# Three early projections in place of six, split gates, and the late modulation's loads and the inversion's writes issued by ACT

## The chip, the cores and the metric

The kernel runs on one core of one Trainium2 chip. The metric is the time of one execution on the device, in microseconds (us). A core has five engines that work at once, each through its own instructions in order: PE (TensorE, matrix products), DVE (VectorE), ACT (ScalarE), POOL (GpSimd) and SP (SyncE). Transfers between device memory (DRAM) and on-chip memory run on 16 DMA engines. They are started by issue instructions, which stand in the order of the engine that issues them: here nearly all on SP.

## The reference, cut to what matters

Two layers over 256 context and 256 latent tokens (512 in all), 2048 channels. Layer 0 mixes with a bidirectional gated DeltaNet, layer 1 with differential attention. Before each layer the tokens are normalised and modulated, `h = rmsnorm(x) * (1 + sc) + sh`, and after it a residual is added with a gate `gt`. The vectors `sh`, `sc`, `gt` are thirds of `silu(c) @ ada_w + ada_b`, a 2048 by 6144 product for each layer and for each of two vectors, `c` and `c_ctx`.

```python
def project(h):
    qkv, z, ba = jnp.split(h @ w_in, [DN_CONV_CH, DN_CONV_CH + DN_VW], axis=-1)
    q, k, v = jnp.split(short_conv_silu(qkv, conv_w), [DN_QK, 2 * DN_QK], axis=-1)
    ...
    beta = jax.nn.sigmoid(ba[:, :, :, 0])
    g = -jnp.exp(a_log) * jax.nn.softplus(ba[:, :, :, 1] + dt_bias)
...
gc = jnp.cumsum(chunks(g), axis=-1)
decay = jnp.exp(gc[..., :, None] - gc[..., None, :])          # lower triangle
lower = strict(einsum(kb, kc) * decay)
tinv = triangular_solve(eye + lower, eye)
a_intra = einsum(qc, kc) * decay
# then a scan over the chunks: v_new = u - w S, o = q S + a_intra v_new, S = ...
```

## The kernel before, in words

**Tiling.** Layer 0 has 16 groups `g` of two value heads. A group needs six projections of the 512 tokens by 128 columns: `k`, `q`, `v0`, `v1`, `z0`, `z1`. Numbers are kept in two parts, a rounded `hi` and a rest `lo` (`split`, line 184: ACT casts the `hi` at line 185, POOL subtracts the `lo` at line 187), and each product is three matmuls. One projection is 16 tiles of the contracted channels times 3, so 48 matmuls of 128x512 on PE; the weights of group 0's `k` are called `g0k…`, and so on.

**Prologue (lines 259 to 325).** A first half of layer 0's modulation (`sh`, `sc`) comes from 64 loads `ar` of 512 KB and 256 groups of small matmuls (`ada_pair`, line 173). `make_h` (line 216) then writes the modulated tokens `hhi`, `hlo`, two tiles a step, POOL first, then ACT, then DVE; its factor `rrow` needs all 16 tiles `xt` of the input. In step with it run six early projections: `ba` (the input of the gates), `k0`, `q0`, `v00`, `v01` and group 1's `k1`. Their weights are loads `er` at line 308, cast and split like the others. The tile `rc` is `silu(c)`, written to DRAM as `sc_d` by an issue on ACT (line 324).

**Gates (line 375).** `gt_baT` takes over the projection `ba` (line 397), PE turns it, and a softplus of both halves at once (tiles 512 wide; reciprocal at line 420, a chain of seven steps at line 425) gives `g` (line 434) and `lnb`. `gc_d` takes the cumulated `g` to DRAM in four writes, and `gct` (line 440, finished at line 459) keeps it on chip. The small table `adt`, which the softplus needs at line 416, is loaded at line 371.

**The steady state.** `decay` (line 677) loads a piece of `gc_d` into the single buffer `grm` or `gra` (line 681), DVE subtracts (line 687), ACT takes the exponential (line 689), and `ma` or `at` (line 695) is a product with it. `block_inv` (line 698) inverts small triangles: it writes `m16` to `mb_d` (line 701), reads it back in another layout as `bk` (line 703), runs 15 steps `bP`, `bY` on DVE (lines 712, 714), casts `bT` on ACT (lines 717, 718) and writes it to `tu_d` (line 720). `stream_lev` (line 755) loads `T` and `U` from there (line 774) and doubles the inverse on PE, up to `uf` (line 790). With `uf`, `stream_b` runs the scan. `filler` (line 647) puts the remaining projections between these.

**Late modulation.** The rest of the modulation (`gt` of layer 0, all of layer 1) is cut into 1024 pieces. `ada_part` (line 133) loads `aw` (line 135, two buffers `ra`), POOL multiplies it by a copy `cr` of `silu(c)` (line 138, one buffer `rp`) and ACT sums the product (line 139). `cr` is loaded from `sc_d` at line 158.

**What sets the order.** Generators describe streams with priorities and model costs; a loop `Drive` (line 481 on) steps the one that is ready. `dr.set("tu", g, half, lat=32)` tells that loop that the inverse is there 32 us later. The framework then schedules the instructions of each engine by its own timeline and high-priority blocks. On the chip every engine keeps the order that came out.

```python
nc.sync.dma_start(r, d["adaw"][l, ct, :, q * NK:(q + 1) * NK])          # line 135
nc.gpsimd.tensor_tensor(pr, r, cr[:, s], ALU.mult)                       # line 138
nc.scalar.activation(pr, pr, AF.Copy, accum_out=acc[:, s, q:q + 1])      # line 139
```

Of the kernel before, what the change touches and what calls it, by code (L numbers as in the profile page):

```python
# [61 lines left out]
def body(ctx, tc, D, d, out):  # L62
# [208 lines left out]
    with tc.high_priority():  # L271
        ada_pair(0, 0, ada_load(0, 0, t0, "ar", 12), gq(), t0)
        xt = [hpool.tile([P, T], F32, tag="hlo", name=f"xt{kt}", bufs=KT) for kt in range(KT)]
        for kt in range(KT):
            nc.sync.dma_start(xt[kt], d["xT"][:, kt])
    with tc.high_priority():
        acc0 = t0.tile([P, T], F32, name="acc0")
        nc.scalar.activation(acc0, xt[0], AF.Square)
        for kt in range(1, KT):
            sq = t0.tile([P, T], F32, tag="mh", name=f"sq{kt}", bufs=2)  # L280
            nc.scalar.activation(sq, xt[kt], AF.Square)
            nc.vector.tensor_tensor(acc0, acc0, sq, ALU.add)
        rrow0 = t0.tile([P, T], F32, name="rrow0")
        nc.scalar.copy(rrow0, rstd_rows(acc0, T, lambda: so().rearrange("p a b i -> p (a b i)"),
                                         t0.tile([P, 4, P], F32, name="rr_dg0")))

    SK = 2
# [7 lines left out]
    np_ = 0  # L295
    for k0 in range(0, KT, SK):
        with tc.high_priority():
            for kind in range(2):
# [6 lines left out]
        for n, src, _ in EARLY:
            w = SK * P
            r = t0.tile([P, w], F32, tag="er", name=f"e{n}r{k0}", bufs=4)
            nc.sync.dma_start(r, src[:, k0 * P:k0 * P + w])
            hi = t0.tile([P, w], F32R, tag="eh", name=f"e{n}h{k0}", bufs=8)
            lo = t0.tile([P, w], F32R, tag="el", name=f"e{n}l{k0}", bufs=8)  # L310
            split(hi, lo, r)
            for k in range(SK):
                kt, ks = k0 + k, slice(k * P, (k + 1) * P)
                ps = early[n]
                mm(ps, hi[:, ks], hhi[:, kt, :], kt == 0, False)
                mm(ps, hi[:, ks], hl(kt), False, False)
                mm(ps, lo[:, ks], hhi[:, kt, :], False, kt == KT - 1)
    rc = t0.tile([2, D], F32, name="rc")
    nc.sync.dma_start(rc, d["crow"])
    rth = t0.tile([2, D], F32, name="rth")  # L320
    nc.scalar.activation(rth, rc, AF.Tanh, scale=0.5)
    nc.vector.scalar_tensor_tensor(rc, rth, 1.0, rc, ALU.add, ALU.mult)
    nc.vector.tensor_scalar(rc, rc, 0.5, None, ALU.mult)
    nc.scalar.dma_start(sc_d, rc)
# [31 lines left out]
    zt = dl.tile([P, 1024], F16, name="zt", tag="m16", bufs=4)  # L356
    nc.vector.memset(zt, 0.0)
    full = lambda a: a.rearrange("u (j i) -> j u i", i=P)[:P]
    diag = lambda a: bass.AP(tensor=a[:].tensor, offset=a[:].offset, ap=[[16 * P + 16, 64], [P, 16], [1, 16]])
    for i in range(2):  # L360
        for j in range(2):
            nc.sync.dma_start(full(tu_d[i][j]), zt.rearrange("p (u i) -> p u i", u=8))

    convw = load_small("convw", [P, 4 * KT, 5], d["convw"], dl)
    adt = load_small("adt", [P, 2, 2, HV], d["adt"].to_broadcast([P, NB]).rearrange("p (k d h) -> p k d h", k=2, d=2), dl)
    hh = lambda kt: hhi[:, kt, :]

    beta = dl.tile([P, NCH, 2, HV], F32, name="beta", tag="O", bufs=2)
    gct = dl.tile([P, NCH, 2, HV], F32, name="gct")
    eg = dl.tile([P, NCH, 2, HV], F32, name="eg")  # L370
    kd = dl.tile([P, NCH, 2, HV], F32, name="kd")
    egl = dl.tile([P, NCH, 2, HV], F32, name="egl")
# [922 lines left out]
```

## Time and profile before

| what | value |
|---|---|
| three runs, median (lowest to highest) | 3181.67 us (3176.39 to 3182.67) |
| the profiled execution, its own time | 3170.24 us |
| its span, first to last instruction | 3168.5 us |
| granted TensorE clock, mean over the span | 0.954 of full speed |
| PE, DVE, POOL, ACT busy | 89%, 62%, 64%, 59% of the span |
| first `uf` (end of the start-up) | 342.2 us |

The page and the answers of the trace are read in microseconds from the first instruction. "A <- B" after a wait names what ended it. A name ending in q (SPq, ACTq) is the engine's queue, where DMAs are issued; "busy" counts no issue time. Matmul records overlap by pipelining, so the distance between their starts tells the rate, and the record's own length does not.

### The profile page before, as it was taken

The page shows a single profiled execution, that of the slowest core. Times are in us where ns is not written, and L with a number is a line of the kernel's source. Part 1 is how long each engine was busy: PE and PEld are TensorE (multiplying, and loading weights), DVE is VectorE, ACT ScalarE, POOL GpSimd, SP SyncE. Part 2 cuts the span into 40 slices and gives each one's busy share as a digit, 9 for nine tenths or more (in the row PEclk, how much of TensorE's full clock was granted, in tenths as well). Part 3 has the DMA queues.
Part 4 walks back from the last instruction along what each step waited for, and adds up shares of the span by engine and source line. Part 5 has one row for each costly group of instructions (what it writes and reads, how often), then busy time and mean ns, then how long its engine had stood idle before and what let it go on. Part 6 is the DMA issues. An engine that isn't in the chain of part 4 may idle for free.

```text
span 3168.5 us, 52448 instructions
## 1 busy us (share of the span) xinstructions
PE 2833.0 (89%) x16178; PEld 2236.6 (71%) x16178; DVE 1980.1 (62%) x4274; ACT 1863.0 (59%) x5466; POOL 2026.2 (64%) x2370
## 2 busy tenths in 40 slices
PE   4977888888998988998988988899898999999998
PEld 1555666676776766776766766677686888888888
DVE  2148768778778688588688688632334664545454
ACT  3545666666766766766666666654455665434354
POOL 2567677777787777777777777566466677322234
PEclk6988999999999999999999999999999999999999
DMA  9645445455545555545455546656744454333345
GB/s 362 223 114 118 123 119 135 123 133 118 139 134 129 127 126 133 128 129 136 122 125 131 132 118 134 173 171 189 230 147 132 144 164 150 123 110 113 117 127 164
DMA packets 511795, 457.06 MB, mean 144 GB/s; under 512 B 241684, under 2 KB 383764, under 8 KB 511508
## 3 DMA queue, kind: packets, MB, share of 16 engines
q1 hardware_dynamic: 511508, 453.68, 51.8%
q8 instruction: 127, 2.08, 0.3%
q14 instruction: 156, 1.28, 0.1%
q10 hardware_dynamic: 4, 0.02, 0.0%
HBM read 427.18 MB, written 26.36 MB: 143 GB/s over the span
## 4 chain that ended last, share of the span: by engine, by line
PE 33%; DVE 26%; DMA 19%; ACT 7%; POOL 7%; issue 5%; SPq 2%; POOLq 0%; DVEq 0%; ACTq 0%
PE pj L83 28%; DMA gra<-gc_d 5%; POOL rp L138 4%; DMA grm<-gc_d 4%; DVE bP L712 4%; DVE grm L687 3%; DMA aw<-in_adaw_dram 3%; DVE gra L687 2%; DVE bY L714 2%; ACT rp L139 2%; DVE R L783 1%; PE sb L83 1%; DMA ar<-in_adaw_dram 1%; PE iv L83 1%; DVE ma L695 1%
## 5 line engine op out<-in xcount | busy, mean ns | idle before, releaser
L139 ACT ACTIVATE rp<-rp 128x256 f32<-128x256 f32 x1024 | 426.9, 417 | 378.6 <-POOL rp L138 375.5
L712 DVE TENSOR_TENSOR bP<-bX,bY 64x1 f32<-64x1 f32 (+14 forms) x480 | 228.8, 477 | 18.1 <-ACT bY L710 9.8
L139 ACT ACTIVATION_READ_ACCUMULATOR rp<-rp 128x1 f32 x1024 | 194.0, 189 | 0.0
L687 DVE TENSOR_SCALAR gra<-gra,gct,lnb 128x128 f32<-128x128 f32 x256 | 114.3, 488 | 97.9 <-DMA gra<-gc_d 97.2
L687 DVE TENSOR_SCALAR grm<-grm,gct,lnb 128x128 f32<-128x128 f32 x256 | 144.9, 610 | 47.9 <-DMA grm<-gc_d 47.3
L783 DVE TENSOR_TENSOR R<-iv,lv 128x512 f16<-128x512 f32 x192 | 126.1, 678 | 32.8 <-PE iv L83 32.6
L689 ACT ACTIVATE grm<-grm 128x512 f32<-128x512 f32 x64 | 40.4, 631 | 132.0 <-DVE grm L687 127.1
L83 PEld LDWEIGHTS <-m 128*128 128x128 f16 x1024 | 74.2, 100 | 62.0 <-issue 57.7
L714 DVE TENSOR_REDUCE bY<-bP 64x1 f32<-64x1 f32 (+14 forms) x480 | 108.8, 227 | 8.7
L83 PE MATMUL iv<-U,R 128*128 128x128 f16 x768 | 75.7, 223 | 34.4 <-DVE R L783 30.0
L83 PEld LDWEIGHTS <-R 128*128 128x128 f16 x768 | 47.6, 99 | 77.6 <-DVE R L783 44.6
L745 POOL TENSOR_TENSOR ma<-ma,cs 128x512 f32<-128x512 f32 x64 | 85.3, 1333 | 20.7 <-DVE ma L695 18.3
L83 PE MATMUL sb<-yb,uf 128*128 128x128 bf16 x512 | 54.2, 225 | 40.7 <-ACT yb L879 22.2
L689 ACT ACTIVATE gra<-gra 128x512 f32<-128x512 f32 x64 | 40.4, 631 | 84.1 <-DVE gra L687 84.1
L83 PE MATMUL iv<-T,m 128*128 128x128 f16 x768 | 71.4, 223 | 15.8 <-ACT T L800 7.2
L224 DVE TENSOR_TENSOR hlo<-mh,hhi 128x512 fp32r<-128x512 f32 x32 | 29.6, 929 | 86.8 <-ACT hhi L223 77.8
L748 POOL TENSOR_TENSOR ml<-ma,m 128x512 bf16<-128x512 f32 x64 | 76.1, 1189 | 10.5 <-ACT m L747 10.3
L83 PEld LDWEIGHTS <-uf 128*128 128x128 f16 x512 | 36.4, 100 | 64.6 <-issue 59.1
L801 ACT CAST U<-iv 128x512 f16<-128x512 f32 x128 | 75.7, 591 | 0.0
L800 ACT CAST T<-iv 128x512 f16<-128x512 f32 x128 | 73.7, 576 | 3.0 <-PE iv L83 2.9
L83 PE MATMUL so<-x,at 128*128 128x128 f32 x512 | 71.6, 280 | 3.8 <-DVE x L911 2.7
L83 PEld LDWEIGHTS so<-x,at 128*128 128x128 f32 x512 | 64.9, 194 | 6.2 <-DVE x L911 3.6
(2758 smaller groups left out, 11429.3 us busy)
## 6 DMA issues: line engine op xcount, KB each, us to landing
aw<-in_adaw_dram SPq DMA_DIRECT2D x512, 128.0 KB, 3.0
ar<-in_adaw_dram SPq DMA_DIRECT2D x64, 512.0 KB, 7.3
gra<-gc_d SPq DMA_DIRECT2D x128, 128.0 KB, 4.2
grm<-gc_d SPq DMA_DIRECT2D x128, 128.0 KB, 4.1
mb_d<-m SPq DMA_DIRECT2D x32, 256.0 KB, 3.7
T<-tu_d SPq DMA_DIRECT2D x128, 64.0 KB, 2.7
U<-tu_d SPq DMA_DIRECT2D x128, 64.0 KB, 2.7
yd<-sz SPq DMA_DIRECT2D x32, 256.0 KB, 3.4
```

The source lines that it names most:

```text
L83: nc.tensor.matmul(o, l, r, start=start, stop=stop)
L138: nc.gpsimd.tensor_tensor(pr, r, cr[:, s], ALU.mult)
L139: nc.scalar.activation(pr, pr, AF.Copy, accum_out=acc[:, s, q:q + 1])
L687: nc.vector.tensor_scalar(gr[:, u], gr[:, u], gct[:, c, dd, j:j + 1], lnb[:, c, dd, j:j + 1], ALU.subtract, ALU.min)
L689: nc.scalar.activation(gr, gr, AF.Exp)
L712: nc.vector.tensor_tensor(pr[:, :i, :i], X[:, i, :i].unsqueeze(1).to_broadcast([64, i, i]), Y[:, :i, :i].rearrange("p j c -> p c j"), ALU. ...
L714: nc.vector.tensor_reduce(Y[:, i, :i], pr[:, :i, :i], AX.X, ALU.add)
L745: nc.gpsimd.tensor_tensor(ma, ma, ident.unsqueeze(1).to_broadcast([P, 4, P]), ALU.add)
L748: nc.gpsimd.tensor_tensor(ml[:, :, k], mv, m16[:, :, k], ALU.subtract)
L783: nc.vector.tensor_tensor(R, quad(pp), lvb(n), ALU.mult)
L800: nc.scalar.copy(Tm, quad(pt))
L801: nc.scalar.copy(U, quad(pu))
```

## The change

1. **Early projections.** Three instead of six: `ba`, `k0`, `q0`. `v00`, `v01` and `k1` become ordinary work of `filler`. The whole prologue is one high-priority block. `xt` is loaded ahead of `ar`; `ar` has 8 buffers instead of 12; `rc` is computed as 128x32 instead of 2x2048, first of all; `convw` and `adt` are loaded within the prologue.
2. **Gates.** The softplus runs in two halves, 256 wide: `g`'s first, then two writes of `gc_d` instead of four, then `lnb`'s. The write of `sc_d` is kept behind `eg`, so the late modulation starts after the gates. The `tu_d` zeros come from a small tile.
3. **ACT's queue.** 512 loads `aw`, 256 loads `cr`, 32 writes `mb_d` and 64 writes `tu_d` are issued by ACT. SP's issues fall from 2506 to 1628, ACT's rise from 1 to 865.
4. **Order.** `stream_lev` no longer waits for group 0's `v`; `stream_at` waits for group 0's inversion; the latency told to `Drive` is 46 instead of 32.

```diff
     def ada_part(l, ct, q, cr, acc, NK):
-        nc.sync.dma_start(r, d["adaw"][l, ct, :, q * NK:(q + 1) * NK])
+        nc.scalar.dma_start(r, d["adaw"][l, ct, :, q * NK:(q + 1) * NK])
...
-                nc.sync.dma_start(cr[:, s], sc_d[s:s + 1, q * NK:(q + 1) * NK].to_broadcast([P, NK]))
+                nc.scalar.dma_start(cr[:, s], sc_d[s:s + 1, q * NK:(q + 1) * NK].to_broadcast([P, NK]))
...
-    EARLY = [("ba", d["wba"], so()), ("k0", d["win"][0, 1], pj()), ("q0", d["win"][0, 0], pj()),
-             ("v00", d["win"][0, 2], iv()), ("v01", d["win"][0, 3], iv())]
-    if G > 1:
-        EARLY.append(("k1", d["win"][1, 1], sb()))
+    EARLY = [("ba", d["wba"], so()), ("k0", d["win"][0, 1], pj()), ("q0", d["win"][0, 0], pj())]
...
+    with tc.high_priority():
+        for kt in range(KT):
+            nc.sync.dma_start(xt[kt], d["xT"][:, kt])
...
+                ada_pair(0, pr, ada_load(0, pr, ta, "ar", 8), (gq, tr)[np_ % 2](), ta)
...
+        convw = load_small("convw", [P, 4 * KT, 5], d["convw"], gp)
+        adt = load_small("adt", [P, 2, 2, HV], ..., gp)
...
-        nc.vector.reciprocal(w2, u2)
-        for k in (15, 13, 11, 9, 7, 5, 3):
-            nc.vector.scalar_tensor_tensor(f5(w2), f5(w2), 2.0 / k, f5(e2), ALU.add, ALU.mult)
+        def softplus(k):
+            nc.vector.reciprocal(w, u)
+            for m in (15, 13, 11, 9, 7, 5, 3):
+                nc.vector.scalar_tensor_tensor(fl(w), fl(w), 2.0 / m, fl(e), ALU.add, ALU.mult)
+            return w
+        w = softplus(1)
+        nc.vector.tensor_tensor(g, w, wide(ea), ALU.mult)
+        for a in range(2):
+            nc.scalar.copy(r.rearrange("p q i -> p (q i)"), p3[:HV])
+            nc.sync.dma_start(gc_d[2 * a:2 * a + 2].rearrange("c (d h) i -> h (c d) i", d=2), r)
+        nc.vector.tensor_scalar(lnb, softplus(0), -1.0, None, ALU.mult)
+        tc.keep_in_program_order(nc.scalar.activation(eg, p1v, AF.Exp))
+        tc.keep_in_program_order(nc.scalar.dma_start(sc_d.rearrange("s (p i) -> (s p) i", i=W2), rc))
...
-        nc.sync.dma_start(full(mb_d[par]), m16.rearrange("p d c h i -> p (d c h) i"))
+        nc.scalar.dma_start(full(mb_d[par]), m16.rearrange("p d c h i -> p (d c h) i"))
...
-            nc.sync.dma_start(diag(tu_d[par][j]), TU[:, j])
+            nc.scalar.dma_start(diag(tu_d[par][j]), TU[:, j])
...
-                dr.set("tu", g, half, lat=32)
+                dr.set("tu", g, half, lat=46)
...
     def stream_lev(p):
-        yield ev("conv", 0, "v0")
-        yield ev("conv", 0, "v1")
...
     def stream_at():
+            if g == 0:
+                yield ev("tu", 0, 1)
```

In the changed file the lines from 280 on stand 3 to 6 further down. On POOL, in the second half of the prologue, these rows stood before (`rp` is a piece of the late modulation, `e…l` the `lo` of an early projection):

```order
55 L138 TENSOR_TENSOR rp_32_10_2831<-aw_32_1_2829,cr(0, 32)1_2826 128x256
56 L187 TENSOR_TENSOR eq0l_766<-eq0r_763,eq0h_765 128x256
57 L187 TENSOR_TENSOR ev00l_778<-ev00r_775,ev00h_777 128x256
58 L187 TENSOR_TENSOR ev01l_790<-ev01r_787,ev01h_789 128x256
59 L138 TENSOR_TENSOR rp_32_11_2834<-aw_32_1_2829,cr(0, 32)1_2826 128x256
60 L187 TENSOR_TENSOR ek1l_802<-ek1r_799,ek1h_801 128x256
61 L187 TENSOR_TENSOR ebal_892<-ebar_889,ebah_891 128x256
62 L138 TENSOR_TENSOR rp_33_10_2839<-aw_33_1_2837,cr(0, 32)1_2826 128x256
63 L187 TENSOR_TENSOR ek0l_904<-ek0r_901,ek0h_903 128x256
64 L187 TENSOR_TENSOR eq0l_916<-eq0r_913,eq0h_915 128x256
```

And now, up to the end of the prologue (`mh` belongs to `make_h`, `g0v0lo` to the first projection after it):

```order
45 L220 TENSOR_TENSOR mh_13_981<-xt_145,rrow_131 128x256 x2
46 L187 TENSOR_TENSOR ebal_1106<-ebar_1103,ebah_1105 128x256
47 L187 TENSOR_TENSOR ek0l_1118<-ek0r_1115,ek0h_1117 128x256
48 L187 TENSOR_TENSOR eq0l_1130<-eq0r_1127,eq0h_1129 128x256
49 L220 TENSOR_TENSOR mh_14_1087<-xt_146,rrow_131 128x256 x2
50 L220 TENSOR_TENSOR mh_15_1095<-xt_147,rrow_131 128x256 x2
51 L187 TENSOR_TENSOR g0v0lo_1316<-g0v0r_1303,g0v0hi_1315 128x256
52 L187 TENSOR_TENSOR g0v0lo_1328<-g0v0r_1325,g0v0hi_1327 128x256
```

Three `lo` splits a step are left of six, and no `rp` stands among them; the first is row 60. On SP, where `adt` was loaded before:

```order
161 L135 DMA aw_35_2_3246<-in_adaw_dram 128x256
162 L135 DMA aw_32_3_3650<-in_adaw_dram 128x256
163 L135 DMA aw_33_3_3658<-in_adaw_dram 128x256
164 L158 DMA cr(0, 32)4_4107<-sc_d 128x256 x2
165 L135 DMA aw_34_3_3666<-in_adaw_dram 128x256
166 L135 DMA aw_35_3_3674<-in_adaw_dram 128x256
167 L100 DMA convw<-in_convw_dram 128x320
168 L100 DMA adt<-in_adt_dram 128x128
169 L362 DMA tu_d_88<-zt 128x8x128
170 L362 DMA tu_d_89<-zt 128x8x128
```

And where it is loaded now:

```order
54 L316 DMA eq0r_443<-in_win_dram 128x256
55 L169 DMA ar_91_379<-in_adaw_dram 128x1024
56 L100 DMA convw<-in_convw_dram 128x320
57 L100 DMA adt<-in_adt_dram 128x128
58 L169 DMA ar_92_385<-in_adaw_dram 128x1024
59 L169 DMA ar_93_391<-in_adaw_dram 128x1024
```

`adt` stood behind all early weights and six loads `aw`; now it stands amid the loads of the prologue. On SP, where group 0's inverse was written and read before:

```order
230 L681 DMA grm_2420<-gc_d 128x256 x2
231 L119 DMA g2kr_3095<-in_win_dram 128x512
232 L720 DMA tu_d_88<-bT_1915 64x16x16
233 L720 DMA tu_d_89<-bT_1915 64x16x16
234 L135 DMA aw_36_1_6522<-in_adaw_dram 128x256
235 L774 DMA T_2332<-tu_d_88 128x2x128 x2
236 L774 DMA U_2333<-tu_d_89 128x2x128 x2
237 L774 DMA T_2338<-tu_d_88 128x2x128 x2
238 L774 DMA U_2339<-tu_d_89 128x2x128 x2
```

And the writes now, on ACT (`m` is `m16`, `g1qhi` casts of a projection's weights):

```order
222 L752 CAST m_1879<-ma_1907 128x2x256
223 L694 ACTIVATE grm_2200<-grm_2200 128x512
224 L185 CAST g0z1hi_1982<-g0z1r_1970 128x256
225 L706 DMA mb_d_87<-m_1879 128x8x128
226 L139 ACTIVATE rp_35_10_2830,al_35_2019<-rp_35_10_2830 128x256
227 L185 CAST g1qhi_1995<-g1qr_1993 128x256
228 L722 CAST bT_1626<-bY_1624 32x256
229 L723 CAST bT_1626<-bY_1624 32x256
230 L722 CAST bT_1626<-bY_1624 32x256
231 L723 CAST bT_1626<-bY_1624 32x256
232 L185 CAST g1qhi_2009<-g1qr_1993 128x256
233 L725 DMA tu_d_89<-bT_1626 64x16x16
234 L725 DMA tu_d_88<-bT_1626 64x16x16
```

The writes `mb_d` and `tu_d` now stand behind the casts that they write out, on the engine that makes the casts; `T` and `U` are still loaded by SP.

## Rows read from the trace of the kernel before

**Rows 1.** The page, part 1: busy time, share of the span and instructions of each engine.

```profile
PE 2833.0 (89%) x16178; PEld 2236.6 (71%) x16178; DVE 1980.1 (62%) x4274; ACT 1863.0 (59%) x5466; POOL 2026.2 (64%) x2370
```

**Rows 2.** The page, part 4: the chain that ended last, by engine and by line.

```profile
PE 33%; DVE 26%; DMA 19%; ACT 7%; POOL 7%; issue 5%; SPq 2%; POOLq 0%; DVEq 0%; ACTq 0%
PE pj L83 28%; DMA gra<-gc_d 5%; POOL rp L138 4%; DMA grm<-gc_d 4%; DVE bP L712 4%; DVE grm L687 3%; DMA aw<-in_adaw_dram 3%; DVE gra L687 2%; DVE bY L714 2%; ACT rp L139 2%; DVE R L783 1%; PE sb L83 1%; DMA ar<-in_adaw_dram 1%; PE iv L83 1%; DVE ma L695 1%
```

**Rows 3.** Stretches: us, PE, PEld, DVE, ACT, POOL busy, clock, DMA share, GB/s.

```profile
0.00:80.00 80.00, 37.24 (x265) 14.24 (x265) 19.24 (x31) 27.08 (x57) 16.91 (x23) 0.64 0.96 359
...
142.00:178.00 36.00, 35.24 (x153) 27.44 (x150) 2.41 (x3) 21.01 (x66) 31.30 (x44) 1.00 0.48 133
...
192.00:237.00 45.00, 31.96 (x117) 24.33 (x118) 33.35 (x38) 22.07 (x78) 27.91 (x33) 0.69 0.33 95
...
342.00:1000.00 658.00, 589.96 (x3470) 455.09 (x3469) 506.40 (x1173) 436.93 (x1367) 492.01 (x614) 0.96 0.51 128
1000.00:2000.00 1000.00, 889.60 (x5247) 686.73 (x5248) 769.15 (x1776) 661.37 (x2060) 747.09 (x925) 0.97 0.52 129
```

**Rows 4.** Timeline of POOL, 150 to 192: start, us, instruction.

```profile
164.31 0.75 POOL L187 TENSOR_TENSOR ebal<-ebar,ebah 128x256 fp32r<-128x256 f32 x1
...
169.52 0.74 POOL L187 TENSOR_TENSOR ek1l<-ek1r,ek1h 128x256 fp32r<-128x256 f32 x1
...
171.23 0.74 POOL L187 TENSOR_TENSOR ebal<-ebar,ebah 128x256 fp32r<-128x256 f32 x1 [0.27 <-ACT ebah L185]
```

**Rows 5.** Timeline of DVE, 175 to 240 (columns as above).

```profile
178.03 0.69 DVE L397 COPY gt_baT<-so 128x512 f32<-128x512 f32 x1 [23.54 <-PE so L83]
...
191.74 0.96 DVE L416 TENSOR_TENSOR gt_t<-gt_ba,adt 128x256 f32<-128x256 f32 x1
...
195.76 3.35 DVE L420 RECIPROCAL gt_w<-gt_u 128x512 f32<-128x512 f32 x1
...
212.61 0.94 DVE L434 TENSOR_TENSOR gt_g<-gt_w,gt_ea 128x256 f32<-128x256 f32 x1
...
215.09 1.75 DVE L451 RECIPROCAL beta<-gt_e 128x256 f32<-128x256 f32 x1
...
236.12 1.00 DVE L459 TENSOR_TENSOR gct<-gct,lnb 128x256 f32<-128x256 f32 x1
```

**Rows 6.** Timeline of SP, 165 to 192: queue instructions, their waits inside their time.

```profile
173.41 7.32 SPq L135 DMA_DIRECT2D aw<-in_adaw_dram  x3
...
186.68 0.42 SPq L100 DMA_DIRECT2D adt<-in_adt_dram  x1
```

**Rows 7.** Tile uf, line 790: ns min/median/max, first and last start in us, forms.

```profile
L790 ACT CAST uf<-iv x64: 560/578/624, 342.2 to 2035.3; 128x512 f16<-128x512 f32 x64
```

**Rows 8.** The chain in order of time, 178 to 345: start, us, what.

```profile
245.21 0.95 PE pj L83 x4
```

**Rows 9.** Waits on SP, 342 to 2000: us in total, times, longest us.

```profile
SPq L135 <- POOL rp L138: 282.8, 203, 4.9
SPq L681 <- DVE ma L695: 67.8, 31, 5.6
```

**Rows 10.** Waits of all engines, 342 to 2000 (columns as above).

```profile
DVE gra L687 <- DMA gra<-gc_d: 94.5, 60, 5.2
...
DVE grm L687 <- DMA grm<-gc_d: 41.5, 33, 4.6
```

**Rows 11.** Lines 135, 158, 701, 720: ns min/median/max, first and last start us.

```profile
L135 SPq DMA_DIRECT2D aw<-in_adaw_dram x512: 327/332/1264, 54.3 to 2687.6; - x171
...
L158 SPq DMA_DIRECT2D cr(0, 32)3_3647<-sc_d x2: 424/424/424, 164.8 to 166.2; - x2
...
L701 SPq DMA_DIRECT2D mb_d<-m x32: 359/378/434, 267.8 to 1940.3; - x32
...
L720 SPq DMA_DIRECT2D tu_d<-bT x64: 580/598/2567, 301.7 to 1978.8; - x64
```

**Rows 12.** The page, part 5: line, engine, names, count | busy, mean ns | idle.

```profile
L139 ACT ACTIVATE rp<-rp 128x256 f32<-128x256 f32 x1024 | 426.9, 417 | 378.6 <-POOL rp L138 375.5
```

More of the change, by code (lines that the diff above doesn't have):

```diff
@@ L258, in so @@
         return psm.tile([P, 2, 2, P], F32, tag="so", name="so", bufs=1)
-    t0_cm = pool("t0")
+    gp_cm = pool("gp", side="right")
+    gp = gp_cm.__enter__()
+    gct, eg, kd, egl, lnb = (gp.tile([P, NCH, 2, HV], F32, name=n) for n in ("gct", "eg", "kd", "egl", "lnb"))
+    zt = gp.tile([P, P], F16, name="zt")
+    nc.vector.memset(zt, 0.0)
+    t0_cm = pool("t0", reuse_waits="tile")
     t0 = t0_cm.__enter__()
@@ L270, in body @@
     nc.vector.tensor_reduce(sel4, ident.rearrange("p (j s) -> p s j", s=32)[:, :2, :], AX.X, ALU.add)
[L271 to L287, printed above, removed]
-    EARLY = [("ba", d["wba"], so()), ("k0", d["win"][0, 1], pj()), ("q0", d["win"][0, 0], pj()),
-             ("v00", d["win"][0, 2], iv()), ("v01", d["win"][0, 3], iv())]
-    if G > 1:
-        EARLY.append(("k1", d["win"][1, 1], sb()))
+    W2 = 2 * D // P
+    rc = gp.tile([P, W2], F32, name="rc")
+    nc.sync.dma_start(rc, d["crow"].rearrange("s (p i) -> (s p) i", i=W2))
+    rth = t0.tile([P, W2], F32, name="rth")
+    nc.scalar.activation(rth, rc, AF.Tanh, scale=0.5)
+    nc.vector.scalar_tensor_tensor(rc, rth, 1.0, rc, ALU.add, ALU.mult)
+    nc.vector.tensor_scalar(rc, rc, 0.5, None, ALU.mult)
+    ta_cm = pool("ta", reuse_waits="tile")
+    EARLY = [("ba", d["wba"], so()), ("k0", d["win"][0, 1], pj()), ("q0", d["win"][0, 0], pj())]
     if NB < P:
@@ L305, in body @@
[L305 to L324, printed above, removed]
+                make_h((xt[kt][:, 0:256], xt[kt][:, 256:512]), kt, rrow0, 0, hhi, hl, ta, nc.gpsimd)
+            for n, src, _ in EARLY:
+                w = SK * P
+                r = ta.tile([P, w], F32, tag="er", name=f"e{n}r{k0}", bufs=6)
+                nc.sync.dma_start(r, src[:, k0 * P:k0 * P + w])
+                hi = ta.tile([P, w], F32R, tag="eh", name=f"e{n}h{k0}", bufs=6)
+                lo = ta.tile([P, w], F32R, tag="el", name=f"e{n}l{k0}", bufs=6)
+                split(hi, lo, r)
+                for k in range(SK):
+                    kt, ks = k0 + k, slice(k * P, (k + 1) * P)
+                    ps = early[n]
+                    mm(ps, hi[:, ks], hhi[:, kt, :], kt == 0, False)
+                    mm(ps, hi[:, ks], hl(kt), False, False)
+                    mm(ps, lo[:, ks], hhi[:, kt, :], False, kt == KT - 1)
@@ L355, in body @@
     dl = dl_cm.__enter__()
[L356 to L372, printed above, removed]
-    lnb = dl.tile([P, NCH, 2, HV], F32, name="lnb")
-    def gates():
-        class t1:
-            @staticmethod
-            def tile(shape, dt, name, tag, bufs=2):
-                return dl.tile(shape, dt, name="gt_" + name, tag=tag, bufs=dict(at=3, x=1, cy=1, jk=1, y=1, grm=1, gra=1, ma=1).get(tag, bufs))
-        if NB < P:
+    def gates(ps):
+        sh = [P, NCH, 2, HV]
+        HOME = dict(t1="at0", bt="at0", e1="at1", u1="at1", w1="at2", t0="at2", e0="O0", u0="O0", w0="O1", g="O1",
+                    raw="x", be="x", beta="y", kt="y", baT="S", r0="kx", r1="ma", ea="gt_ea", z="at0")
+        homes = {}
+        def tl(name, shape):
+            h = HOME[name]
+            tag, bufs = h.rstrip("012"), {"a": 3, "O": 2}.get(h[0], 1)
+            if len(shape) != 4 or shape[1] != NCH:
+                return dl.tile(shape, F32, name="gt_" + name, tag=tag, bufs=bufs)
+            if h not in homes:
+                homes[h] = [dl.tile([P, 2] + sh[1:], F32, name="gt_" + h, tag=tag, bufs=bufs), 0]
+            t, k = homes[h]
+            homes[h][1] += 1
+            return t[:, k]
+        if ps is None:
@@ L427, in gates @@
-        nc.vector.scalar_tensor_tensor(f5(w2), f5(t2), 0.0, f5(w2), ALU.max, ALU.add)
-        nc.vector.tensor_scalar(lnb, w2[:, 0], -1.0, None, ALU.mult)
-        e, t, w = e2[:, 0], t2[:, 0], w2[:, 1]
-        ea = t1.tile([P, 2, HV], F32, name="ea", tag="jk", bufs=1)
+        t2 = [tl(f"t{k}", sh) for k in range(2)]
+        bt = tl("bt", sh)
+        nc.vector.tensor_tensor(t2[1], ba[:, :, :, 1, :], wide(adt[:, 1]), ALU.add)
+        nc.vector.tensor_copy(bt, ba[:, :, :, 0, :])
+        ea = tl("ea", [P, 2, HV])
@@ L450, in gates @@
+        nc.scalar.activation(egl, p1[:, n:2 * n].rearrange("p (c d h) -> p c d h", c=NCH, d=2), AF.Exp)
+        raw = tl("raw", sh)
+        nc.vector.tensor_copy(raw, p1v)
+        nc.vector.tensor_tensor(gct, raw, lnb, ALU.subtract)
+        e = tl("be", sh)
+        nc.scalar.activation(e, bt, AF.Exp, scale=-1.0)
         nc.vector.tensor_scalar(e, e, 1.0, None, ALU.add)
+        beta = tl("beta", sh)
         nc.vector.reciprocal(beta, e)
-        p2 = sp()
-        mm(p2[:, :n], ones, fl(g))
@@ L463, in conv_silu @@
+    full = lambda a: a.rearrange("u (j i) -> j u i", i=P)[:P]
+    diag = lambda a: bass.AP(tensor=a[:].tensor, offset=a[:].offset, ap=[[16 * P + 16, 64], [P, 16], [1, 16]])
+    for i in range(2):
+        for j in range(2):
+            nc.sync.dma_start(full(tu_d[i][j]), zt.unsqueeze(1).to_broadcast([P, 8, P]))
     def conv_silu(ps, ci, nm):
```

99 lines of the change are left out of this document (48 added, 51 removed).

## The prediction

> **What bounds the kernel now.** I read the page first, then stretches, then the timelines of the stretches that the change touches, then the waits of the steady state. PE is busy 89% of the span [rows 1], and the chain of waits gives PE only 33%, DVE 26% and DMA 19% [rows 2]: much of PE's work lies beside a chain that runs through others, so time can be won where PE is idle. The stretches say where that is [rows 3]. In the first 80 us the DMA engines are the limit, with a share of 0.96 at 359 GB/s and PE busy 37 of 80 us. From 192 to 237 PE is busy 32 of 45 us, at a granted clock of 0.69. From 342 on it is busy 90% (589.96 of 658 us) and 89% (889.60 of 1000 us). So the start-up, up to the first `uf` at 342.2 us [rows 7], is the place with room, and the steady state has a tenth.
>
> From 142 to 178 POOL is busy 31.30 of 36 us, while the DMA share has fallen to 0.48 [rows 3]. A prologue step goes from 164.31 to 171.23 us on POOL [rows 4]: 6.92 us for six `lo` splits and three pieces `rp`. The gates follow on DVE: `gt_baT` at 178.03, but the first operation with `adt` at 191.74, since `adt` was issued at 186.68 [rows 6], behind loads `aw` of which three took 7.32 us on SP. Then a serial chain gives `g` at 212.61 and `gct` at 236.12 [rows 5].
>
> **Edit 1, early projections.** 145 projection matmuls instead of 289 stand ahead of the gates' transposes in PE's order. On POOL three splits a step are left and the `rp` among them are gone; at about 0.7 us each a step's splits take 2.1 us, so POOL stops being the limit. The limit is then the loading: by the sizes in the code 33.6 MB of `ar`, 4.2 of `xt`, 3.1 of early weights and some 3 of the rest, 44 MB, at 359 GB/s [rows 3] 122 us. I add 18 us for the start and for the last two steps, at most 6.92 us each as before: `gt_baT` at 140, **38 us earlier**. The near end is 130. The far end is 160: PE now waits for all `xt` and their sums before its first `ar` product, with 8 buffers instead of 12 behind it, and in the first 80 us it ran at a clock of 0.64 [rows 3]. What was removed is moved, not dropped: up to the first `uf` PE's order has 529 projection matmuls instead of 603, so 74 are left for later. Four take 0.95 us [rows 8], so the debt is 74 × 0.24 = **17.6 us**.
>
> **Edit 2, gates and small loads.** `adt` comes within the prologue: 13.7 us between `gt_baT` and the first use become some 3, **11 us**. The softplus halves its width: the reciprocal of 512 took 3.35 us and that of 256 (for `beta`) 1.75 [rows 5], so the 20.9 us from 191.74 to 212.61 become about 12: **9 us**. From `g` to `gct` 23.5 us passed [rows 5]; the second softplus takes 9 and the tail some 7, beside the two `gc_d` writes: **7 us**. `gct` would come 38 + 11 + 9 + 7 = 65 us earlier, at 172. From there to `uf` it took 105.1 us before (237.1 to 342.2). In this stretch PE now has 384 matmuls, 92 us, instead of the 314 that it had from 178 to 342; I take 8 us back for that: `uf` at 285, **57 us earlier**, and after the debt **40 us gained**. Ends: 10 (prologue at 160, PE the limit after it) and 65. The narrower `rc` stands off the path of the modulation, and the zeros of `tu_d` only have to be there before the first inverse is written, beside 100 us of other work: nothing; without that cover each write is one DMA issue.
>
> **The late modulation** starts after `eg`. In ACT's order 78 of its 1024 pieces stood ahead of the first `uf`, now 27. The 51 move behind; the work is the same, and POOL is busy 75% and ACT 66% of the steady state [rows 3]. I cost it at nothing; if POOL and ACT gave no cover, 51 × 0.74 = 38 us of POOL would return.
>
> **Edit 3, ACT's queue.** SP loses 864 issues. In 342 to 2000 it stood 282.8 us at line 135, waiting for POOL, 1.4 us at a time [rows 9], 17% of that time; every `gra` or `grm` load, `T`, `U` and weight behind it waited too. DVE waited 94.5 + 41.5 = 136 us for those two loads [rows 10], so this lies on the path where DVE does. But the buffer is single: SP also waits for DVE to free it (67.8 us for `ma` [rows 9]), and the transfer itself remains. Of some 240 loads 17% come on a held SP and lose half of 1.4 us or more, 28 us in all; 93 of them had DVE waiting [rows 10], so I take **12 us gained**; ends 0 and 136.
>
> ACT gets the issues: 512 × 0.332 + 256 × 0.424 + 32 × 0.378 + 64 × 0.598 = 170 + 109 + 12 + 38 = 329 us [rows 11]. With 1863 busy [rows 1] that is 69% of the span: no bound, but ACT works in order, and what follows an issue waits. An `aw` stands right behind the sum of the piece whose product last read its buffer; what it waits for is done, and its 332 ns can pass while the sum before it runs 417 ns [rows 12]. `mb_d` and `tu_d` must wait for ACT's own cast just ahead: 50 us in all that nothing hides on ACT. Behind them stand weight casts, exponentials and `yb`. ACT holds 7% of the chain [rows 2]; of 329 us that is 23, of 50 it is 4. I take **8 us lost**; ends 0 and 329. The Trainium skill, "DMA: Bandwidth & Descriptors", section "Issuing engines are not separate DMA queues", says that issuing from several engines saves the sequencer's issue time alone, since all of them share the 16 DMA engines. By it this edit would bring nothing, as SP's queue has 2% of the chain; the rows above speak of waits held in order, of which the rule says nothing.
>
> **Edit 4** shifts the order by some microseconds a group; I cost it at zero, within the range: with 46 for 32 PE meets `T` later and waits less, and the scan of a group may start later.
>
> **Sum.** −40 − 12 + 8 = −44 us. The profiled execution took 3170.24 us, 11.4 below the median of the runs, 3181.67; 3170.24 − 44 = 3126, and on the median's scale 3181.67 − 44 = **3138 us**. A measurement of this kernel can tell some 0.2%, 6.4 us, from no change.
>
> **Rivals.**
> (a) *ACT's order costs more* (slower). For: 865 issues on an engine that feeds PE with casts. Against: 34% idle time in the steady state, and waits that are done when the issue comes. The gains are 52 us, so it decides once more than 52/329 = 16% of the issue time lands on the path. At 40%: 132 − 52 = +80, 3262 us. Chance 0.18.
> (b) *The start-up's gain is given back.* PE's debt and the 51 pieces are paid where POOL and ACT are full: 40 − 38 = 2, with 4 net from edit 3: 3176 us, no change that can be told. For: POOL at 75%, `rp` of lines 138 and 139 with 6% of the chain [rows 2]. Against: the pieces have the whole span to fit in. Chance 0.20.
> (c) *SP was the real brake.* If most of DVE's 136 us of waiting for `gra` and `grm` goes, say 75, with 40 from the start and little lost on ACT: 3181.67 − 115 = 3067 us. For: the two loads hold 9% of the chain. Against: a single buffer. Chance 0.12.
> (d) *The prologue is no shorter than its PE work allows*, `gt_baT` at 160 instead of 140: 20 us less gain, 3158 us. For: the slow clock early. Chance 0.15, inside the range.
> My forecast without these has 0.35.
>
> **How the numbers follow.** (c) down to 3067 and the main cases up to 3205, which takes in some of (a), leave out about 2 in 10: the upper part of (a), 0.13, and the lower part of (c), 0.05. Faster by over 0.2%: 0.35 + 0.15 + 0.12 and 0.06 of (b): 0.68. Within 0.2%: 0.11 of (b): 0.11. Slower: (a) and the remaining 0.03 of (b): 0.21.
>
> **What would show it.** Right: `gt_baT` near 140, first `adt` operation within 4 us of it, `gct` near 172, `uf` near 285; waits of SP at line 135 gone from its list; DVE's waits for `gra` and `grm` below 136 us; the last `uf` some 44 us before 2035.3 [rows 7]. Wrong: `gt_baT` past 160 with PE busy throughout (d); `uf` early, but the end of the steady state where it was (b); PE waiting for ACT's casts, or ACT idle behind its queue's DMAs, for 100 us and more in the steady state (a).

## The result and the profile after

The changed kernel takes **3129.33 us** (median of 4 runs, 3120.79 to 3138.53) where the kernel before takes 3179.03 us (4 runs, 3172.59 to 3182.67): a ratio of 0.985 with a 95% interval of 0.983 to 0.987, 50 us less. The forecast was 44 us less, 3138 on the earlier median of 3181.67. The size was right. The places were largely not, as the experiments show.

The profiled execution of after took 3130.73 us, close to its median; that of before, 3170.24, lay 9 us under its own. So the two traces show 40 of the 50 us, and differences between traces below some 10 us are not read as causes here.

The stretches of the changed kernel that answer to [rows 3], same columns:

```profile
0.00:80.00 80.00, 44.43 (x292) 22.35 (x293) 16.62 (x36) 31.86 (x71) 23.24 (x35) 0.84 0.97 340
...
142.00:178.00 36.00, 28.49 (x121) 22.39 (x122) 28.63 (x48) 13.40 (x31) 6.99 (x9) 0.86 0.15 41
...
192.00:237.00 45.00, 39.45 (x178) 30.21 (x177) 30.68 (x61) 24.25 (x77) 39.23 (x47) 0.96 0.43 107
...
342.00:1000.00 658.00, 589.87 (x3505) 460.29 (x3503) 499.38 (x1166) 432.14 (x1336) 483.86 (x602) 0.96 0.53 128
1000.00:2000.00 1000.00, 885.22 (x5208) 685.97 (x5208) 740.18 (x1736) 659.25 (x2022) 724.33 (x903) 0.96 0.51 128
```

From 142 to 178 POOL is busy 6.99 us instead of 31.30, DVE 28.63 instead of 2.41: the gates run there now. From 192 to 237 PE is busy 39 of 45 us instead of 32. From 342 on nothing of note has changed: 589.87 and 885.22 us of PE, beside 589.96 and 889.60. The gates on DVE, beside [rows 5]:

```profile
149.90 0.69 DVE L392 COPY gt_baT<-so 128x512 f32<-128x512 f32 x1 [4.73 <-PE so L83]
151.75 0.41 DVE L402 TENSOR_TENSOR gt_at<-gq,adt 128x256 f32<-128x256 f32 x1
...
169.04 0.84 DVE L425 TENSOR_TENSOR gt_O<-gt_at,gt_ea 128x256 f32<-128x256 f32 x1
...
181.31 0.42 DVE L449 TENSOR_TENSOR gct<-gt_x,lnb 128x256 f32<-128x256 f32 x1
...
187.49 2.38 DVE L692 TENSOR_SCALAR grm<-grm,gct,lnb 128x128 f32<-128x128 f32 x4
```

The step from `gt_baT` to the first operation with `adt` (line 402) takes 1.9 us where it took 13.7, and `gct` is finished at 181.7 instead of 237.1. The first and last `uf`, and the last product with one (beside [rows 7]; columns: ns min/median/max, first and last start in us):

```profile
L83 PE MATMUL sb<-yb,uf x512: 216/219/330, 302.6 to 2087.6; 128*128 128x128 bf16 x171
L793 ACT CAST uf<-iv x64: 562/584/599, 297.9 to 2019.3; 128x512 f16<-128x512 f32 x64
```

The first `uf` comes 44 us earlier and the last 16; the last product with `yb` was at 2127.3 us before, so it comes 40 us earlier, and the span ends 40 us earlier. Waits on SP in 300 to 1960 us of the changed kernel, beside [rows 9] (us in total, times, longest us):

```profile
SPq L686 <- DVE at L700: 90.8, 37, 6.2
SPq L708 <- DMA mb_d<-m: 74.7, 21, 8.4
SPq L686 <- DVE ma L700: 64.2, 27, 4.9
SPq L777 <- DMA tu_d<-bT: 58.3, 18, 9.9
```

And DVE's waits for the two loads in the same stretch, beside [rows 10]:

```profile
DVE gra L692 <- DMA gra<-gc_d: 76.2, 48, 4.2
DVE grm L692 <- DMA grm<-gc_d: 73.9, 42, 5.9
```

SP's wait at line 135 is gone, as forecast. But DVE waits 76 + 74 = 150 us for `gra` and `grm`, where it waited 136: nothing of the forecast's 12 us is to be seen in this kernel. SP now stands before the same loads because the single buffer is in use (line 686), and before `bk` and `T` because the transfer that they read has not landed (lines 708, 777).

### The profile page after: what moved, and what is told of

It reads as the page before. It is cut to its first block, busy times and chain, and to the rows that moved or that the text cites. A ratio compares the mean times of both kernels' runs of the same rounds, so it can differ in the third digit from the quotient of the medians.

```text
span 3128.9 us, 52162 instructions
## 1 busy us (share of the span) xinstructions
PE 2817.8 (90%) x16178; PEld 2239.7 (72%) x16178; DVE 1955.8 (63%) x4287; ACT 1872.4 (60%) x5466; POOL 2012.8 (64%) x2370
## 5 line engine op out<-in xcount | busy, mean ns | idle before, releaser
L692 DVE TENSOR_SCALAR grm<-grm,gct,lnb 128x128 f32<-128x128 f32 x256 | 133.2, 563 | 84.8 <-DMA grm<-gc_d 84.1
L83 PE MATMUL sb<-yb,uf 128*128 128x128 bf16 x512 | 55.5, 225 | 32.5 <-DVE yb L910 20.9
L803 ACT CAST T<-iv 128x512 f16<-128x512 f32 x128 | 74.1, 579 | 16.2 <-PE iv L83 12.5
```

The source lines that it names most:

```text
L83: nc.tensor.matmul(o, l, r, start=start, stop=stop)
L692: nc.vector.tensor_scalar(gr[:, u], gr[:, u], gct[:, c, dd, j:j + 1], lnb[:, c, dd, j:j + 1], ALU.subtract, ALU.min)
L803: nc.scalar.copy(Tm, quad(pt))
```

## The experiments

Theory 1 is the prediction's: the start-up carries the gain, ACT's queue little. Its rivals: SP was the brake (2), ACT's order costs (3), the early projections alone made the start-up long (4), what only moves the start-up forward is given back (5), the late modulation's pieces ahead of the gates were the cost, by their POOL and ACT time (6). The groups of runs stood on chips on which the kernel before took 3165 to 3180 us, so each kernel is compared by its ratio to the kernel before on the same chip. The last two columns come from one trace of each kernel, on different chips; since the chips differ by up to 15 us over the whole span, differences of some 10 us in the last column are not read.

| kernel | made from | ratio (95% interval) | first `uf`, us | last product with `uf`, us |
|---|---|---|---|---|
| before | | 1 | 342.2 | 2127.3 |
| after | | 0.985 (0.983 to 0.987) | 297.9 | 2087.6 |
| a_rep | after, once more | 0.985 (0.983 to 0.987) | 298.9 | 2085.7 |
| b_actq | before + ACT's queue | 0.999 (0.998 to 1.000) | 355.1 | 2132.0 |
| b_early3 | before + three early projections | 1.000 (0.999 to 1.001) | 319.1 | 2127.3 |
| b_adt | before + early `adt` | 0.996 (0.995 to 0.997) | 347.3 | 2137.0 |
| b_ga | before + early `adt` + split gates | 0.997 (0.995 to 0.998) | 340.8 | 2130.0 |
| b_defer | before + late modulation behind the gates | **0.988** (0.986 to 0.989) | 320.0 | 2094.6 |
| a_spq | after − ACT's queue | 0.992 (0.991 to 0.994) | 292.0 | 2104.4 |
| a_early6 | after, six early projections | 0.986 (0.984 to 0.988) | 308.0 | 2074.1 |
| a_sc0 | after, late modulation from the start | **0.991** (0.989 to 0.992) | 318.8 | 2108.6 |
| a_order | after − edit 4 | 0.984 (0.983 to 0.986) | 301.2 | 2076.4 |
| a_aw_sp | after, `aw`, `cr` on SP | 0.985 (0.984 to 0.987) | 290.6 | 2073.8 |
| a_mbtu_sp | after, `mb_d`, `tu_d` on SP | 0.983 (0.982 to 0.985) | 295.1 | 2079.8 |

**b_actq: the queue alone.** In the kernel before:

```diff
-        nc.sync.dma_start(r, d["adaw"][l, ct, :, q * NK:(q + 1) * NK])
+        nc.scalar.dma_start(r, d["adaw"][l, ct, :, q * NK:(q + 1) * NK])
```

and the same for `cr`, `mb_d` and `tu_d`.

> The kernel before with part 3 alone: the aw and cr loads and the mb_d and tu_d writes issued by ACT, 865 issues in all. Theory 1 (the prediction: the start-up carries the gain, the queue 4 us net): 3175 us, within 12 us of the kernel before; gt_baT near 178 and the first uf near 340 as before; SP's wait at line 135 gone; DVE's waits for gra and grm some 12 us lower. Theory 2 (SP was the brake): 3130 to 3150, with DVE's waits for gra and grm halved from 136 us. Theory 3 (ACT's order costs): over 3195.

Measured: 0.999, 2 us of 3165. Theories 2 and 3 fall as whole explanations. SP's wait at line 135 went, and DVE's waits for `gra` and `grm` mostly did not (waits over the whole span of b_actq):

```profile
DVE gra L687 <- DMA gra<-gc_d: 82.3, 59, 3.7
DVE grm L687 <- DMA grm<-gc_d: 57.1, 45, 3.7
```

139 us in all, against 144.5 over the whole span of the kernel before; from 342 to 2000 us it is 127.6 against 136, so 8 of the 12 us that were forecast. Relieving SP moves most of its wait from POOL to the buffer. The start-up missed the expectation: `gt_baT` came at 184.8 instead of 178 and the first `uf` at 355.1, 13 us later. On ACT two issues of `cr` now stand ahead of prologue work, and a copy behind them (at 105.71) waited 7.3 us. From the first `uf` to the last product with one it took 1776.9 us instead of 1785.1. So the 2 us may be a loss in the start-up and a gain behind it.

**a_spq: the queue taken out of the change.**

```diff
-        nc.scalar.dma_start(r, d["adaw"][l, ct, :, q * NK:(q + 1) * NK])
+        nc.sync.dma_start(r, d["adaw"][l, ct, :, q * NK:(q + 1) * NK])
```

and so for the other three.

> The changed kernel with part 3 undone: the same four kinds of DMA issued by SP again. Theory 1: 3133 us (4 more than the changed kernel), first uf within 8 us of 298. Theory 2: 3155 to 3180, most of the 50 us lost. Theory 3: 3090 to 3115, faster than the changed kernel.

Measured: 0.992. The queue is worth 0.7% (some 23 us) in the changed kernel, between theories 1 and 2, though it was worth nothing alone. The first `uf` did not move the wrong way (292.0 us), so what is lost is lost behind it. The next two runs halve this edit.

**a_aw_sp and a_mbtu_sp: the queue by halves.**

```diff
-        nc.scalar.dma_start(r, d["adaw"][l, ct, :, q * NK:(q + 1) * NK])
+        nc.sync.dma_start(r, d["adaw"][l, ct, :, q * NK:(q + 1) * NK])
...
-                nc.scalar.dma_start(cr[:, s], ...)
+                nc.sync.dma_start(cr[:, s], ...)
```

> The changed kernel with the aw and cr loads (768 issues) back on SP, mb_d and tu_d still on ACT. If the loads that wait for POOL on SP are what ACT's queue relieves: ratio 0.990 to 0.993, as with all four kinds back (0.9923), and SP's wait at line 135 back at some 500 us. If it is the inversion's writes: 0.985.

```diff
-        nc.scalar.dma_start(full(mb_d[par]), m16.rearrange("p d c h i -> p (d c h) i"))
+        nc.sync.dma_start(full(mb_d[par]), m16.rearrange("p d c h i -> p (d c h) i"))
...
-            nc.scalar.dma_start(diag(tu_d[par][j]), TU[:, j])
+            nc.sync.dma_start(diag(tu_d[par][j]), TU[:, j])
```

> The changed kernel with the mb_d and tu_d writes (96 issues) back on SP, aw and cr still on ACT. If the loads are what ACT's queue relieves: ratio 0.985 or a little less, since ACT loses the 50 us of issues that nothing hides. If it is the inversion's writes: 0.990 to 0.993.

Measured: 0.985 and 0.983. Either half can go back without loss; only both together cost. In the first, SP waits at line 135 as it did in the kernel before, and more (waits on SP, whole span of a_aw_sp):

```profile
SPq L135 <- POOL rp L138: 519.5, 397, 6.8
```

The same view of a_spq:

```profile
SPq L135 <- POOL rp L138: 503.5, 398, 5.1
...
SPq L725 <- ACT bT L723: 62.2, 29, 5.4
```

So that wait by itself costs nothing, 519.5 us of it. What differs in a_spq is that SP also waits for the casts `bT` (62.2 us). That wait by itself costs nothing either: a_mbtu_sp has it alone, 90.2 us of it. Whether the two waits in one queue hold each other's followers, or whether the schedule that came out for a_spq is a poor one for another reason, no run here tells apart.

**b_early3 and a_early6: the number of early projections.**

```diff
-    EARLY = [("ba", d["wba"], so()), ("k0", d["win"][0, 1], pj()), ("q0", d["win"][0, 0], pj()),
-             ("v00", d["win"][0, 2], iv()), ("v01", d["win"][0, 3], iv())]
-    if G > 1:
-        EARLY.append(("k1", d["win"][1, 1], sb()))
+    EARLY = [("ba", d["wba"], so()), ("k0", d["win"][0, 1], pj()), ("q0", d["win"][0, 0], pj())]
```

in the kernel before, and the three entries put back in the changed one.

> The kernel before with three early projections instead of six, nothing else. Theory 1: the prologue's POOL has three lo splits less in each of 8 steps, 24 x 0.7 = 17 us; gt_baT near 160 instead of 178, first uf some 15 us earlier, 17 us of PE work left for later: in sum 0 to -15 us, 3165 to 3179. Theory 2: no change, 3179. A theory 4 (the early projections alone made the start-up long): -30 or more, uf before 315.

> The changed kernel with six early projections again. Theory 1: gt_baT 10 to 20 us later than 150 (24 more lo splits on POOL, but no rp among them), uf 5 to 15 us later than 298, 17 us of debt gone: 3120 to 3135 us, near the changed kernel. Theory 4: 3150 or more, uf after 325.

Measured: 1.000 and 0.986. In both directions the step that I counted on most is worth nothing that can be told, and theory 4 falls. The traces show where it goes. Tile `uf` in b_early3 (last two times: first and last start):

```profile
L787 ACT CAST uf<-iv x64: 563/584/624, 319.1 to 2048.3; 128x512 f16<-128x512 f32 x64
```

And in a_early6:

```profile
L794 ACT CAST uf<-iv x64: 562/581/611, 308.0 to 2005.0; 128x512 f16<-128x512 f32 x64
```

Three early projections bring the first `uf` 23 us forward in the kernel before (342.2 to 319.1), and the stretch from first to last `uf` grows from 1693.1 to 1729.2 us. In the changed kernel it is 1697.0 us with six and 1721.4 with three, with first `uf` at 308.0 and 297.9. What the start gains is given back in the steady state, with the debt and more: theory 5 holds for this edit.

**b_adt: the early load of `adt` alone.**

```diff
+    adt = load_small("adt", [P, 2, 2, HV], ..., gp)
     t0_cm = pool("t0")
...
-    adt = load_small("adt", [P, 2, 2, HV], ..., dl)
```

with `convw` beside it.

> The kernel before with adt and convw loaded among the first loads, nothing else. Theory 1: the 13.7 us between gt_baT and the first operation with adt fall to 3, gct and the first uf 8 to 11 us earlier, and the time falls by as much, ratio 0.9965 to 0.998. Theory 5 (what only moves the start-up forward is given back in the steady state, as with three early projections in the kernel before): first uf earlier, ratio 0.999 to 1.001.

Measured: 0.996, yet the first `uf` is no earlier. The gap that I priced at 11 us is still there. DVE waits for ACT now, no longer for the load (timeline of DVE in b_adt):

```profile
179.43 0.69 DVE L399 COPY gt_baT<-so 128x512 f32<-128x512 f32 x1 [20.32 <-PE so L83]
190.89 0.67 DVE L434 TENSOR_SCALAR gt_ea<-gt_ea 128x64 f32<-128x64 f32 x1 [10.78 <-ACT gt_ea L433]
```

and ACT, which needs only `adt` for `gt_ea`, has a run of the late modulation's sums ahead of it, one every 1.35 us, each waiting for POOL (timeline of ACT in b_adt):

```profile
188.87 0.42 ACT L139 ACTIVATE rp<-rp 128x256 f32<-128x256 f32 x1 [0.84 <-POOL rp L138]
...
190.21 0.42 ACT L139 ACTIVATE rp<-rp 128x256 f32<-128x256 f32 x1 [0.83 <-POOL rp L138]
...
190.62 0.24 ACT L433 ACTIVATE gt_ea<-adt 128x64 f32<-128x64 f32 x1
```

In the kernel before, two waits ended at about the same time, that of the sums at 187.7 us and the load's at 189.6 (timelines of DVE and of ACT in the kernel before):

```profile
189.90 0.20 DVE L432 TENSOR_SCALAR gt_ea<-gt_ea 128x64 f32<-128x64 f32 x1 [11.19 <-ACT gt_ea L431]
...
189.62 0.26 ACT L431 ACTIVATE gt_ea<-adt 128x64 f32<-128x64 f32 x1 [1.89 <-DMA adt<-in_adt_dram]
```

The load was named for the last 1.89 us only, and I priced the load alone. Nor is the late modulation's move alone enough: in b_defer the gap is 9.0 us, with PE's transposes as the last wait, where about 4 was expected. In a_sc0, with the early load and with the pieces in their old place, it is 2.0 us. So it takes the order of the changed kernel as a whole. Where the 0.4% come from, the profile doesn't show.

**b_ga: early `adt` and split gates.** The gates of the change, with its `gp` pool, in the kernel before; prologue, late modulation and queues stay.

```diff
-    gates()
+    gates(early.get("ba"))
```

> The kernel before with the early adt and the split gates of the change (two gc_d writes, half-wide softplus), prologue, late modulation and queues as before. Theory 1: 27 us of the forecast's start-up terms (11 + 9 + 7): first uf near 315, ratio 0.9915. Theory 5: first uf near 315 but ratio 0.997 or more. Theory 6 (the late modulation behind the gates is what paid): ratio near 0.997, first uf above 325.

Measured: 0.997, like b_adt without the gates. `gct` is finished 18 us earlier than in b_adt (221.6 against 240.2 us), the first `uf` 6.5 us, the time not at all. The trace of b_ga has 632 projection matmuls ahead of the first `uf`, that of b_adt 592 (some records are missing from both). That PE's work rather than `gct` set the first `uf` there is argued from this, not shown.

**a_sc0 and b_defer: the late modulation's place.** In the changed kernel the write of `sc_d` put first (`eg` then stands where the schedule puts it); in the kernel before put behind `eg`, with `rc` held as 128x32 (ACT's operation on it then takes 0.22 us instead of 1.91):

```diff
     nc.vector.tensor_scalar(rc, rc, 0.5, None, ALU.mult)
+    nc.scalar.dma_start(sc_d.rearrange("s (p i) -> (s p) i", i=W2), rc)
...
-        tc.keep_in_program_order(nc.scalar.dma_start(sc_d.rearrange("s (p i) -> (s p) i", i=W2), rc))
```

> The changed kernel with sc_d written first of all, so that 73 pieces of the late modulation instead of 27 stand ahead of the first uf on ACT. The forecast took the move of the pieces at nothing: ratio 0.983 to 0.987, as the changed kernel. Theory 6: the pieces cost the start-up their POOL and ACT time: first uf 20 to 40 us later, ratio 0.990 to 0.998.

```diff
-    nc.scalar.dma_start(sc_d, rc)
...
-        nc.scalar.activation(eg, gct, AF.Exp)
+        tc.keep_in_program_order(nc.scalar.activation(eg, gct, AF.Exp))
+        tc.keep_in_program_order(nc.scalar.dma_start(sc_d.rearrange("s (p i) -> (s p) i", i=W2), rc))
```

> The kernel before with the write of sc_d kept behind eg on ACT (rc held as 128x32), so that the late modulation starts after the gates; six early projections, one softplus, queues as before. Theory 6 (the pieces among the prologue and ahead of the gates held the start-up): gt_baT near 160 instead of 178, the gap to the first operation with adt near 4 us instead of 13.7, first uf 315 to 325, ratio 0.990 to 0.994, as the 22 us that the same pieces cost in the changed kernel. Theory 5 (given back): first uf earlier, ratio 0.998 or more.

Measured: 0.991 and 0.988. This is the edit that pays most: 0.6% (19 us by the ratios, 22 by the medians) where it is undone, 1.2% (3168.54 to 3131.76, 37 us, more than expected) where it is done alone. I had put it at nothing. It is not the whole: a_sc0, without it, is still 0.9% faster than the kernel before, and no run shows which of the other edits together bring that. In b_defer `gt_baT` comes at 160.2 instead of 178.0 with the same six early projections. In a_sc0 it comes at 175.8 instead of 149.7.

What moved is not only the pieces. The write of `sc_d` is itself an issue on ACT, and in the kernel before it stands directly ahead of the copy `rrow`, on which all modulated tiles wait. ACT did nothing from 56.35 us until it went out, though PE had finished what `rrow` copies at 57.7 (timeline of ACT in the kernel before; "DMA ar" is the landing that ended the wait, and why the write should wait for it the profile doesn't show):

```profile
72.00 0.50 ACTq L324 DMA_DIRECT2D sc_d<-rc  x1
72.54 0.59 ACT L284 COPY rrow<-so 128x512 f32<-128x512 f32 x1 [16.20 <-DMA ar<-in_adaw_dram]
```

In b_defer nothing stands there:

```profile
56.78 0.58 ACT L287 COPY rrow<-so 128x512 f32<-128x512 f32 x1
```

`rrow` comes 15.8 us earlier, `gt_baT` 17.8. The four kernels that keep the write in its old place (b_actq, b_early3, b_adt, b_ga) have the same wait before `rrow`, 15.6 to 18.7 us. In a_sc0 the write goes out at 22.06, but now the first load `cr` waits on ACT, and the copy `arow` behind it runs 15.6 us later than in a_rep (33.19), of the 26 us that `gt_baT` is late:

```profile
48.37 0.33 ACTq L158 DMA_DIRECT2D cr(0, 32)0_2421<-sc_d  x1
48.80 0.37 ACT L178 COPY arow<-tr 128x256 f32<-128x256 f32 x1 [18.25 <-DMA ar<-in_adaw_dram]
```

POOL's time, on the other hand, was not what held `gt_baT` at the end of the prologue: PE had no idle time there in the kernel before (columns of [rows 3]):

```profile
160.00:180.00 20.00, 20.00 (x88) 16.08 (x87) 0.69 (x1) 10.29 (x35) 18.18 (x27) 1.00 0.50 137
```

Where do the pieces go? POOL's instructions of line 138 by stretch (us, busy and count, clock, DMA share, GB/s), first of the kernel before:

```profile
0.00:150.00 150.00, 7.30 (x10) 0.81 0.84 303
150.00:190.00 40.00, 14.77 (x20) 0.99 0.46 126
...
342.00:2000.00 1658.00, 484.77 (x608) 0.96 0.52 128
...
2700.00:3163.00 463.00, 0.00 (x0) 1.00 0.40 124
```

Of b_defer:

```profile
0.00:150.00 150.00, 0.00 (x0) 0.94 0.86 309
150.00:190.00 40.00, 0.00 (x0) 0.89 0.24 67
...
342.00:2000.00 1658.00, 481.62 (x600) 0.96 0.52 129
...
2700.00:3126.00 426.00, 29.48 (x34) 0.99 0.43 132
```

Of a_rep, the changed kernel:

```profile
0.00:150.00 150.00, 0.00 (x0) 0.84 0.84 299
150.00:190.00 40.00, 2.19 (x3) 0.87 0.27 73
...
342.00:2000.00 1658.00, 458.65 (x580) 0.96 0.52 129
...
2700.00:3123.00 423.00, 36.36 (x44) 0.99 0.43 134
```

Of the 30 pieces of the first 190 us none (in a_rep 3) are left there, and 34 (in a_rep 44) now stand behind 2700 us, where none stood. The steady state carries no more of them (608, 600, 580). So the work left the start-up and ended in the last stretch, the differential attention, where POOL is busy 180 of 428 us in the changed kernel, these pieces included. In the gates the pieces may have cost time: from the first operation with `adt` to the finished `gct` it took 45.4 us before and 36.8 in b_defer, 32.0 in a_rep and 36.1 in a_sc0.

That the edit pays is shown in both directions, and theory 5 does not hold here. Theory 6 is right about the edit, and its cause is not shown: the issue that held ACT and the pieces moved with the same line, and no run moves one without the other. Up to `gt_baT` the traces speak for the issue, with 15.8 of 17.8 us.

**a_order: edit 4 undone.**

```diff
-                dr.set("tu", g, half, lat=46)
+                dr.set("tu", g, half, lat=32)
```

with the waits for group 0's `v` put back and that of `stream_at` taken out.

> The changed kernel without edit 4: 32 instead of 46 told for the inversion, group 0's inverse waits for the convolutions of v again, and stream_at for group 0 for nothing. The forecast took the edit at zero: ratio 0.983 to 0.987. Rival: the order is worth 10 us or more, ratio 0.988 and above.

Measured: 0.984, no difference from the changed kernel, as forecast. **a_rep**, the changed kernel as reference of its group:

> The changed kernel once more, beside the three others on one chip, as their reference: ratio 0.985 to the kernel before, as first measured.

Measured: 0.985.

## Why the prediction was right, and where it was not

**The size was right: −44 forecast, −50 measured**, within the range and faster. By its steps:

- *Edit 1, `gt_baT` 38 us earlier.* It came 28 us earlier, at 149.9: the loading up to 142 us moved 80 × 340 + 62 × 284 GB/s = 44.8 MB, as summed, but at less than the 359 GB/s I used throughout. The cause was misread. The prediction took POOL, busy 31.30 of 36 us, for the limit from 142 to 178, where the same row has PE busy 35.24; and it did not see that `rrow` had waited 16.2 us behind an issue on ACT. With six early projections and that issue behind the gates (b_defer) `gt_baT` comes at 160.2. As for the time, three projections for six are worth nothing (b_early3, a_early6): the debt of 17.6 us was right in kind and too small, since first to last `uf` grew by 24 to 36 us.
- *Edit 2, 11 + 9 + 7 us.* The gap before the first operation with `adt` shrank by 11.9 us, but the load alone does not do it (15.4 us in b_adt). The half-wide softplus gave 3.6 us for 9: from the first operation with `adt` to `g` 17.3 us instead of 20.9, as DVE puts convolution steps between. `g` to the finished `gct` took 12.7 us instead of 24.5, 12 gained for 7. The three add up to the forecast's 27 us by luck, since two of them were far off. In time the gates brought nothing that a run shows (b_ga against b_adt).
- *First `uf` 57 us earlier.* It came 44 us earlier: 10 of the missing 13 lie at `gt_baT`, 3 between `gct` and `uf`, which took 116 us instead of 105 where 113 was forecast. The last `uf`, expected some 44 us earlier, came 16 earlier.
- *The late modulation at nothing.* **This is the step that failed.** The prediction argued that 51 pieces merely move behind, and gave their return a rival's chance (38 us given back). It saw the same pieces take three of nine places in POOL's prologue step, and booked that gain under the early projections. The runs show 19 to 37 us for this step alone. And it has no term for what the traces show as the larger part up to `gt_baT`: the write of `sc_d`, which moved too, had held ACT for 16.2 us ahead of `rrow`.
- *Edit 3, −12 + 8.* Net −4 forecast, about −2 alone (b_actq), and 23 in the changed kernel, which either half of the edit secures. The reason given, earlier `gra` and `grm` loads, shows in b_actq (8 us less waiting) and not in the changed kernel, where DVE waits 150 us for them instead of 136. That ACT's issues cost little held in sum: an issue whose wait is over runs beside ACT's own work, as a row further down shows, while one that must wait holds ACT (7.3 us in b_actq). The rule of the Trainium skill ("DMA: Bandwidth & Descriptors", section "Issuing engines are not separate DMA queues"), that such a move saves issue time alone, agrees with b_actq's 2 us; the 23 us are not covered by it.
- *Edit 4 at zero* held (a_order).

Of the rivals, (a) is refuted as a forecast of the time: 865 issues cost nothing in sum that can be told. (b) is right for the early projections and wrong for the pieces. (c) is refuted. (d) came half way by its number, 149.9 between 140 and 160; its cause does not show, as PE was busy 97 of the first 142 us.

So a right total came from terms of which the largest was booked to the wrong edit: that the sum came out is in good part luck. What stays open is how the gain of the late modulation's move divides between the issue that held ACT and the pieces' own time, what brings a_sc0's 0.9%, why the queue edit is worth 23 us only as a whole and only in the changed kernel, and where b_adt's 0.4% arise.

## What to carry to other kernels

A DMA issue is an instruction in the order of the engine that issues it. While its wait lasts, everything behind it on that engine waits too: one write of 16 KB ahead of `rrow` held ACT, and with it the prologue, for 16 us, and the profile puts that wait down to the copy behind it. So look, in a start-up, for idle time of an engine that ends at an issue. Moving 50 of 1024 pieces of POOL and ACT work, with the write that starts them, from the start-up towards the end of the program brought more than shortening the chain of the start-up itself. A start-up that ended earlier by pushing PE work into a steady state that is 90% full gained nothing, in both directions tried. Before a wait is priced, look at what else would end at the same moment: an in-order engine with other work ahead of the same instruction is a second wait, which the row with the last one does not name.
